# Indices of block 2 transposed earlier, block 3's weights ordered behind block 4's dots, two small loads moved to POOL

## The chip, the cores and the metric

The kernel runs on one core of a Trainium2 chip. The metric is the time of one execution in device microseconds, median of three runs. The engines are TensorE (PE), VectorE (DVE), ScalarE (ACT), GpSimd (POOL) and SyncE (SP). Each works through its own instructions in a fixed order and waits where an input or a buffer isn't ready; everything behind a waiting instruction waits with it. Sixteen DMA engines move what the queues of SP, ACT and POOL issue.

## The reference, cut to what matters

One layer of a hybrid decoder for 512 prompt tokens and 8 samples. Two token mixers come first and are not touched. Behind them stands a channel mixer, PEER, and the change lies wholly in it. For each token and each of 8 heads it picks 16 of 16384 experts, so 128 a token:

```python
s1, i1 = lax.top_k(s[:, :, 0], 16); s2, i2 = lax.top_k(s[:, :, 1], 16)   # two key halves
eidx = i1 * 128 + i2                       # best 16 pairs a head, 128 experts a token
g    = softmax(top_s)
act  = gelu(einsum('nd,nhkd->nhk', x, u[eidx]))          # a dot with 128 rows of u
y    = x1 + einsum('nhk,nhkd->nd', g * act, v[eidx])     # a weighted sum of 128 rows of v
```

All is float32, a row of `u` or `v` is 4 KB, and `u` and `v` hold 64 MB each.

## The kernel before, in words

The prompt's 512 tokens make four blocks of 128: blocks 1 and 2 (`halves[0]`, in the code also A) and blocks 3 and 4 (`halves[1]`, also B). The part that matters here runs from about 1075 us to the end and has these pieces:

- **Gather and dot** (`gather_dot`, L1107 to L1122). For each k of 128, POOL issues an indirect DMA that fetches one row of `u` for each of the 128 tokens (512 KB, tile `urow`, L1115), and DVE takes the dot with the token's own row `xn2` (L1122) into column k of `S`. `urow` comes from a ring of 6 slots. `xn2` has one buffer, so block 4's can only be loaded (on SP's queue, L1110) once block 3's last dot is done. `gelu_w` (L1132 to L1138) then turns `S` into weights.
- **Weights as a matrix** (`w_block`, L1161 to L1192). For blocks 1 to 3, rows of `v` are not gathered. The 128 weights of each token are spread over all 16384 experts: per token one one-hot over `i1` scaled by the weight and one over `i2`, and their product on PE gives a 128 x 128 table `WT`. 32 groups of 4 tokens; in each DVE makes `ohe` (L1173), DVE and POOL scale it (`oh`, L1178, L1176), ACT makes the other one-hot (L148, L1183), PE multiplies (`ps_w`, L1190), and ACT copies to `WT` (L151). Ahead of the groups `w_prep` (L1146) transposes `i1`, `i2` and `S` on PE (L1150) and copies them with ACT to `T_i1`, `T_i2`, `T_n2` (negated) and `T_S`, one buffer each. Block 3's `WT` tiles take the slots of block 1's.
- **Dense passes** (`v_part`, L1194 to L1200). SP loads 128 rows of `v` at a time (`vtile`, 512 KB, 5 slots) and PE multiplies them with `WT`. Pass 1: row tiles 0 to 63 for block 1. Pass 2: 64 to 127 for blocks 1 and 2. Pass 3: 0 to 63 for blocks 2 and 3. Pass 4: 64 to 127 for block 3. After the last matmul of a block `v_done` (L1203) adds the residual `x1r` on DVE (L1207) and stores.
- **Block 4 by gather** (`v_rows_acc`, L1210 to L1218). Beside passes 3 and 4, POOL gathers block 4's rows of `v` (L1214, tiles `vslab` and `vrow`) and DVE adds them into an accumulator (L1216), which lies in lane 0 of `slab[0]` and starts as the residual, loaded on SP's queue (L1211). The first 32 rows alternate between ring slots and 7 lanes of the slab.
- **Samples** (`sample_peer`, L1220 to L1263). The 8 samples' dots (`urow_s`, `xb`) are strewn among block 4's, their `v` rows (`vrow_s`) among block 4's rows. Their residual `x1s` takes one of the five `v` slots (L1259), is loaded by SP (L1260), added and stored.

Program order and engine order are not the same. A planner fixes each engine's order when the kernel is built: it plays the program through with durations of its own and lets each engine take the first ready instruction in program order. `tc.issue_after(x)` lets those instructions of its body which are on the engine of x follow x. Before, pass 1 carries such an anchor: block 2's `w_block` stays behind the matmuls of row tile 27 on PE (`JW`), and block 4's rows follow its last `urow` on POOL. On the chip the order stays, while the durations differ from the planner's.

The order of the program around the change: `w_block` of block 1, the top-16 search of block 4 (`late`), gather of block 3 with pass 1, `w_block` of block 2, pass 2, gather of block 4, `w_block` of block 3, pass 3, pass 4 with block 4's rows.

Of the kernel before, what the change touches and what calls it, by code (L numbers as in the profile page):

```python
# [15 lines left out]
P = 128  # L16
# [35 lines left out]
BPE, NPE = (4, 4), (4, 2)  # L52
EQD = (5, 6)
EARLY = True
JH, JC, JW = 64, 0, 27
SLOPES = [2.0 ** (-(h + 1)) for h in range(8)]


def step_kernel(
# [1048 lines left out]
    def gather_dot(d, tok, off, steps, every):  # L1108
        xn2 = keep.tile([P, D], F32, tag="xn2", name="xn2", bufs=1)
        nc.sync.dma_start(xn2, scr_xn2[tok:tok + P])  # L1110
        for k in range(P):
            if steps and k % every == 0:
                next(steps, None)
            gt = ring.tile([P, D], F32, tag="g", name="urow")
            d["rows"] = nc.gpsimd.indirect_dma_start(  # L1115
                out=gt, out_offset=None, in_=u_rows,
                in_offset=bass.IndirectOffsetOnAxis(ap=d["e"][:, k:k + 1], axis=0))
            if off and k % off == off - 1:
                nc.gpsimd.tensor_mul(gt, gt, xn2)
# [23 lines left out]
    def w_new(*pools):  # L1143
        return [(pool.tile([P, JH, P], F32, tag="WT", name="WT", bufs=2), JH * i) for i, pool in enumerate(pools)]

    def w_prep(sel, pool, pst_):  # L1146
        out = []
        for key in ("i1", "i2", "S"):
            p = pst_()
            nc.tensor.transpose(p[:, 0:P], sel[key], ident)  # L1150
            t = pool.tile([P, P], BF16 if key == "i1" else F32, tag=f"T_{key}", name=f"T_{key}", bufs=1)
            copy(t, p[:, 0:P])
            out.append(t)
            if key == "i2":
                t = pool.tile([P, P], F32, tag="T_n2", name="T_n2", bufs=1)
                copy(t, p[:, 0:P], scale=-1.0)
                out.append(t)
        return out

    iota4 = []  # L1160

    def w_block(sel, wT, pool, pst_, no):
        ONA, PM = ONAS[no], PMS[no]
        if not iota4:
            t = pool.tile([P, P, TG], BF16, name="iota4")
            nc.vector.tensor_copy(t, iota.unsqueeze(2).to_broadcast([P, P, TG]))
            iota4.append(t)
        i1T, i2T, ni2T, sT = w_prep(sel, pool, pst_)
        for g in range(P // TG):
            t0 = g * TG  # L1170
            tg = slice(t0, t0 + TG)
            e = pool.tile([P, P, TG], BF16, tag="ohe", name="ohe", bufs=OHE)
            nc.vector.tensor_tensor(e, iota4[0], i1T[:, tg].unsqueeze(1).to_broadcast([P, P, TG]), op=ALU.is_equal)  # L1173
            a = pool.tile([P, TG, P], F32, tag="oh1", name="oh1", bufs=OH1)
            sb = sT[:, tg].unsqueeze(2).to_broadcast([P, TG, P])
            nc.gpsimd.tensor_mul(a[:, :PM], e.rearrange("p j t -> p t j")[:, :PM], sb[:, :PM])  # L1176
            if PM < TG:
                nc.vector.tensor_mul(a[:, PM:], e.rearrange("p j t -> p t j")[:, PM:], sb[:, PM:])  # L1178
            b = pool.tile([P, TG, P], F32, tag="oh2", name="oh2", bufs=OHB)
            for t in range(ONA):  # L1180
                act(b[:, t, :], iota, AF.Abs, bias=ni2T[:, t0 + t:t0 + t + 1])
            if ONA:
                nc.scalar.activation(b[:, 0:ONA, :], b[:, 0:ONA, :], AF.Relu, bias=one, scale=-1.0)  # L1183
            if ONA < TG:
                n = TG - ONA
                nc.vector.tensor_tensor(b[:, ONA:TG, :], iota.unsqueeze(1).to_broadcast([P, n, P]),
                                        i2T[:, t0 + ONA:t0 + TG].unsqueeze(2).to_broadcast([P, n, P]), op=ALU.is_equal)
            pw = pst_().rearrange("p (t j) -> p t j", t=TG)
            for t in range(TG):
                nc.tensor.matmul(pw[:, t, :], b[:, t, :], a[:, t, :], start=True, stop=True)  # L1190
            for w, j0 in wT:
                copy(w[:, :, t0:t0 + TG], pw[:, :, j0:j0 + w.shape[1]].rearrange("p t j -> p j t"))  # L1192

    def v_part(j, use):  # L1194
        vt = dv[0].tile([P, D], F32, tag="v", name="vtile", bufs=VB)
        nc.sync.dma_start(vt, v_rows[j * P:(j + 1) * P])
        for py, wT, j0, j1 in use:
            w = next(w[:, j - b, :] for w, b in wT if b <= j < b + w.shape[1])
            for q in range(2):
                mm = nc.tensor.matmul(py[q], w, vt[:, q * 512:(q + 1) * 512], start=(j == j0), stop=(j == j1))  # L1200
        return mm

    def v_done(tok, py):  # L1203
        t = dv[0].tile([P, D], F32, tag="v", name="x1r", bufs=VB)
        nc.sync.dma_start(t, scr_x1[tok:tok + P])
        for q in range(2):
            nc.vector.tensor_add(t[:, q * 512:(q + 1) * 512], t[:, q * 512:(q + 1) * 512], py[q])  # L1207
        nc.scalar.dma_start(y_prompt[0, tok:tok + P], t)

    def v_rows_acc(d, tok, acc, slot):  # L1210
        nc.sync.dma_start(acc, scr_x1[tok:tok + P])  # L1211
        for k in range(P):
            gt = slot()
            nc.gpsimd.indirect_dma_start(out=gt, out_offset=None, in_=v_rows,  # L1214
                                         in_offset=bass.IndirectOffsetOnAxis(ap=d["e"][:, k:k + 1], axis=0))
            nc.vector.scalar_tensor_tensor(acc, gt, d["S"][:, k:k + 1], acc, op0=ALU.mult, op1=ALU.add)  # L1216
            yield
        nc.gpsimd.dma_start(y_prompt[0, tok:tok + P], acc)  # L1218

    def sample_peer(py):  # L1220
# [30 lines left out]
        for b in range(NS):  # L1251
# [15 lines left out]
    for hf in range(2):  # L1267
# [50 lines left out]
        if hf == 1:  # L1318
            alt = [0]

            def pst_w():
                alt[0] ^= 1
                return pst("ao"[alt[0]])

            wA0 = w_new(wr, wr)
            w_block(halves[0][0][0], wA0, wr, pst_w, 0)
            late()
            py = []
            steps = sample_peer(py)
# [100 lines left out]
```

## Time and profile before

| | us |
|---|---|
| median of 3 runs | 2266.93 (2264.25 to 2271.74) |
| the profiled execution | 2271.8 |
| its span | 2270.1 |
| PE, DVE, POOL, ACT busy | 1977.4, 1536.7, 1307.7, 655.4 |
| mean DMA rate over the span | 310 GB/s |

The profile is of one execution. Times in its rows count from the start of the span. A "DMA share" is the mean busy share of the 16 DMA engines; where they are never idle it reads 1.03. In brackets behind an instruction stands how long its engine was idle before it, and what ended that. A float32 matmul appears as two records.

### The profile page before, as it was taken

What the parts mean: (1) busy time and instruction counts of PE and PEld (TensorE: products, weight loads), DVE (VectorE), ACT (ScalarE), POOL (GpSimd) and SP (SyncE); (2) the same over time, 40 slices, a digit from 0 to 9 for tenths busy, and PEclk for the clock granted to TensorE, in tenths of its full rate; (3) what the DMA queues carried; (4) which work ended last, traced back from release to release, by engine and by line L of the source; (5) the groups of instructions that cost most, each with busy time, mean ns of one, the idle gap of its engine ahead of it and who ended that gap; (6) DMA issues with size and microseconds to landing.
All of it is one profiled execution on the core that took longest, in us unless ns stands there. A gap on an engine that the chain in (4) does not pass through costs nothing. (4 is left out here: it accounts for less than half of the span.)

```text
span 2270.1 us, 25459 instructions
## 1 busy us (share of the span) xinstructions
PE 1977.4 (87%) x7694; PEld 1312.6 (58%) x7694; DVE 1536.7 (68%) x3504; ACT 655.4 (29%) x1775; POOL 1307.7 (58%) x1226
## 2 busy tenths in 40 slices
PE   6999999888989999899897984989999699986817
PEld 4675777777878777787775732634445544431202
DVE  2355576787698977777886698855626856536694
ACT  3343233311344433334534315910014600000000
POOL 0487783453486645676776377554415854545573
PEclk9997999999988999999997997999999699997959
DMA  5685776889698889999988297899969899999999
GB/s 158 199 271 203 236 242 214 276 281 325 221 323 286 299 280 340 343 355 340 325 313 321 87 347 262 309 380 409 409 238 355 279 404 409 409 376 417 417 392 369
DMA packets 297803, 704.78 MB, mean 310 GB/s; under 512 B 31518, under 2 KB 157530, under 8 KB 297666
## 3 DMA queue, kind: packets, MB, share of 16 engines
q0 software_dynamic: 114224, 415.84, 49.1%
q1 hardware_dynamic: 183010, 285.74, 35.8%
q10 hardware_dynamic: 432, 1.57, 0.2%
q8 instruction: 61, 1.00, 0.2%
q14 instruction: 76, 0.62, 0.1%
HBM read 684.87 MB, written 18.18 MB: 310 GB/s over the span
## 5 line engine op out<-in xcount | busy, mean ns | idle before, releaser
L1115 POOL DMA_INDIRECT urow<-in_peer_u,k_e x512 | 602.2, 1176 | 394.9 <-DVE urow L1122 279.5
L1122 DVE SCALAR_TENSOR_TENSOR urow<-urow,xn 128x1024 f32<-128x1024 f32 x512 | 643.7, 1267 | 176.4 <-DMA urow<-in_peer_u,k_e 171.7
L1200 PE MATMUL y<-vtile,WT 128*128 128x512 f32 x1024 | 467.4, 601 | 73.6 <-DMA vtile<-in_peer_v 73.1
L291 PE MATMUL ps_mm<-x,wch 128*128 128x264 f32 (+1 forms) x1536 | 384.0, 403 | 27.5 <-DVE sig L315 20.2
L1200 PEld LDWEIGHTS y<-vtile,WT 128*128 128x128 f32 x1024 | 192.2, 192 | 337.5 <-issue 230.2
L291 PEld LDWEIGHTS ps_mm<-x,wch 128*128 128x128 f32 x1536 | 300.4, 200 | 83.9 <-DVE sig L315 23.5
L835 POOL TENSOR_TENSOR kpage<-kpage,qb 128x1024 f32<-128x1024 f32 x64 | 150.2, 2360 | 72.1 <-DMA qb<-scr_q 64.7
L291 PE MATMUL ps_mm<-hT,wch 128*128 128x256 f32 (+1 forms) x768 | 184.8, 390 | 3.9 <-DVE sig L315 3.6
L1214 POOL DMA_INDIRECT vslab<-in_peer_v,k_e x112 | 131.6, 1175 | 87.2 <-DMA vslab<-in_peer_v,k_e 37.7
L1216 DVE SCALAR_TENSOR_TENSOR vslab<-vslab,k_S 128x1024 f32<-128x1024 f32 x112 | 143.9, 1285 | 44.6 <-DMA vslab<-in_peer_v,k_e 41.9
L291 PEld LDWEIGHTS ps_mm<-hT,wch 128*128 128x128 f32 x768 | 143.1, 193 | 26.4 <-DVE sig L315 4.0
L1200 PE MATMUL ps_a<-vtile,WT 128*128 128x512 f32 x256 | 135.4, 611 | 18.4 <-DMA vtile<-in_peer_v 18.3
L296 PE MATMUL ps_mm<-wch,x 128*128 128x256 f32 (+1 forms) x640 | 150.0, 386 | 0.0
L823 POOL DMA_INDIRECT vpage<-in_cache_v,kidx x64 | 79.1, 1236 | 107.6 <-DVE vacc L901 68.1
L1200 PE MATMUL ps_o<-vtile,WT 128*128 128x512 f32 x256 | 132.3, 599 | 0.0
L296 PEld LDWEIGHTS ps_mm<-wch,x 128*128 128x128 f32 (+1 forms) x640 | 108.0, 174 | 29.5 <-issue 2.8
L901 DVE SCALAR_TENSOR_TENSOR vacc<-vpage,aS,vacc 128x128 f32<-128x128 f32 x384 | 110.6, 359 | 18.6 <-DMA vpage<-in_cache_v,kidx 18.4
L148 ACT ACTIVATE oh<-iota,T_n 128x128 f32<-128x128 f32 x352 | 113.4, 403 | 0.1
L1190 PE MATMUL ps_w<-oh,oh 128*128 128x128 f32 x512 | 81.1, 313 | 31.6 <-POOL oh L1176 23.9
L1190 PEld LDWEIGHTS ps_w<-oh,oh 128*128 128x128 f32 x512 | 74.3, 219 | 52.1 <-POOL oh L1176 33.6
L1176 POOL TENSOR_TENSOR oh<-ohe,T_S 128x128 f32<-128x128 bf16 (+1 forms) x96 | 69.7, 733 | 53.2 <-ACT T_S L151 37.3
L836 DVE TENSOR_REDUCE sK<-kpage 128x16 f32<-128x1024 f32 x64 | 77.3, 1211 | 29.1 <-POOL kpage L835 29.0
(428 smaller groups left out, 2728.1 us busy)
## 6 DMA issues: line engine op xcount, KB each, us to landing
vtile<-in_peer_v SPq DMA_DIRECT2D x256, 512.0 KB
wch<-in_w_in SPq DMA_DIRECT2D x256, 256.0 KB
wch<-in_peer_wq SPq DMA_DIRECT2D x64, 256.0 KB
wch<-in_w_branch_a SPq DMA_DIRECT2D x32, 256.0 KB
wch<-in_w_branch_b SPq DMA_DIRECT2D x32, 256.0 KB
wch<-in_w_out SPq DMA_DIRECT2D x32, 256.0 KB
urow<-in_peer_u,k_e POOLq DMA_INDIRECT x512, 7.9
qb<-scr_q SPq DMA_DIRECT2D x8, 512.0 KB
```

The source lines that it names most:

```text
L148: nc.scalar.activation(out, in_, func, bias=b[:n, 0:1] if b.shape[0] != n else b, scale=scale, **kw)
L291: nc.tensor.matmul(out, w[:, c0:c0 + m], xk[:, :n], start=(k == 0 and i == 0), stop=(k == KT - 1 and i == len(tt) - 1))
L296: nc.tensor.matmul(out, x[:, k, t0:t0 + m], ch[k // KP][:, k % KP, :n], start=(k == 0), stop=(k == KT - 1))
L823: nc.gpsimd.indirect_dma_start(out=t, out_offset=None, in_=rows, in_offset=bass.IndirectOffsetOnAxis(ap=kidx[:, b * 8 + pg:b * 8 + pg + 1] ...
L835: (nc.vector if KDV and pg % KDV == KDV - 1 else nc.gpsimd).tensor_mul(kt, kt, qb)
L901: nc.vector.scalar_tensor_tensor(acc[:, h, :], vt[:, h, :], wa, acc[:, h, :], op0=ALU.mult, op1=ALU.add)
L1115: d["rows"] = nc.gpsimd.indirect_dma_start(out=gt, out_offset=None, in_=u_rows, in_offset=bass.IndirectOffsetOnAxis(ap=d["e"][:, k:k + 1], ...
L1122: d["dot"] = nc.vector.scalar_tensor_tensor(gt, gt, 1.0, xn2, op0=ALU.mult, op1=ALU.mult, accum_out=d["S"][:, k:k + 1])
L1190: nc.tensor.matmul(pw[:, t, :], b[:, t, :], a[:, t, :], start=True, stop=True)
L1200: mm = nc.tensor.matmul(py[q], w, vt[:, q * 512:(q + 1) * 512], start=(j == j0), stop=(j == j1))
L1214: nc.gpsimd.indirect_dma_start(out=gt, out_offset=None, in_=v_rows, in_offset=bass.IndirectOffsetOnAxis(ap=d["e"][:, k:k + 1], axis=0))
L1216: nc.vector.scalar_tensor_tensor(acc, gt, d["S"][:, k:k + 1], acc, op0=ALU.mult, op1=ALU.add)
```

## The change

- `w_prep` takes a list of what to transpose and keeps the results in the block's record; the tiles have two buffers each. `T_n2` is gone: ACT computes |i2 - iota| with scale -1 and bias `T_i2` in place of |iota - i2|.
- Block 2's three transposes stand right behind block 1's `w_block` (so ahead of `late` and of pass 1's anchor). Block 3's `i1` and `i2` stand ahead of block 4's gather; its `S` stays in `w_block`.
- Block 3's `w_block` gets two anchors: its DVE instructions follow block 4's dot 24, its POOL instructions follow block 4's gather 30 (both counted from 0).
- Block 4's accumulator is a tile of its own in the buffer of `xn2`, loaded by POOL. The samples' `x1s` is a tile of the ring, loaded by POOL.
- The split between passes is named `NA` (64) and no longer `JH` (64).

```diff
-JH, JC, JW = 64, 0, 27
+JH, JC, JW, NA, HB = 64, 0, 27, 64, (24, 30)
...
-    def w_prep(sel, pool, pst_):
-        out = []
-        for key in ("i1", "i2", "S"):
+    def w_prep(sel, pool, pst_, keys=("i1", "i2", "S")):
+        T = sel.setdefault("T", {})
+        for key in keys:
             p = pst_()
             nc.tensor.transpose(p[:, 0:P], sel[key], ident)
...
+            T[key] = pool.tile([P, P], BF16 if key == "i1" else F32, tag=f"T_{key}", name=f"T_{key}", bufs=2)
+            copy(T[key], p[:, 0:P])
...
-        i1T, i2T, ni2T, sT = w_prep(sel, pool, pst_)
+        w_prep(sel, pool, pst_, [k for k in ("i1", "i2", "S") if k not in sel.get("T", {})])
+        i1T, i2T, sT = (sel["T"][k] for k in ("i1", "i2", "S"))
...
-                act(b[:, t, :], iota, AF.Abs, bias=ni2T[:, t0 + t:t0 + t + 1])
+                act(b[:, t, :], iota, AF.Abs, scale=-1.0, bias=i2T[:, t0 + t:t0 + t + 1])
...
     def v_rows_acc(d, tok, acc, slot):
-        nc.sync.dma_start(acc, scr_x1[tok:tok + P])
+        nc.gpsimd.dma_start(acc, scr_x1[tok:tok + P])
...
-        x1s = dv[0].tile([NS, D], F32, tag="v", name="x1s", bufs=VB)
-        nc.sync.dma_start(x1s, scr_x1s)
+        x1s = ring.tile([NS, D], F32, tag="g", name="x1s")
+        nc.gpsimd.dma_start(x1s, scr_x1s)
...
             w_block(halves[0][0][0], wA0, wr, pst_w, 0)
+            w_prep(halves[0][0][1], wr, pst_w)
             late()
...
     v_done(0, useA0[0])
+    w_prep(selB[0], wr, pst_d, ("i1", "i2"))
     gather(1, 1, lambda: wr.tile([P, P], F32, name="ge_y", bufs=1),
            (next(steps) if k % 8 == 4 and k < 68 else None for k in range(P)))
     wB0 = w_new(wr, wr)
-    w_block(selB[0], wB0, wr, pst_d, 2)
+    with tc.issue_after(selB[1]["dots"][HB[0]].ins), tc.issue_after(selB[1]["gets"][HB[1]].ins):
+        w_block(selB[0], wB0, wr, pst_d, 2)
...
-    run = v_rows_acc(selB[1], HALF + P, slab[0][:, 0, :], gslot)
+    acc = keep.tile([P, D], F32, tag="xn2", name="acc", bufs=1)
+    run = v_rows_acc(selB[1], HALF + P, acc, gslot)
```

## Rows read from the trace of the kernel before

**Rows 1.** Windows: us, busy time by engine (instructions), PE clock, DMA share, GB/s.
```profile
1380.00:1400.00 20.00, 4.60 (x7) 2.15 (x8) 13.53 (x31) 8.58 (x26) 17.38 (x18) 0.52 0.47 148
...
1660.00:1670.00 10.00, 10.00 (x24) 4.37 (x23) 0.00 (x0) 0.00 (x0) 0.00 (x0) 1.00 0.53 190
1670.00:1680.00 10.00, 10.00 (x25) 4.43 (x24) 0.00 (x0) 0.00 (x0) 0.00 (x0) 1.00 0.43 152
1680.00:1690.00 10.00, 10.00 (x26) 4.45 (x25) 0.43 (x1) 0.28 (x1) 0.38 (x1) 1.00 0.54 205
1690.00:1700.00 10.00, 10.00 (x37) 5.46 (x36) 7.80 (x14) 4.21 (x12) 5.07 (x6) 1.00 0.42 140
...
1960.00:2000.00 40.00, 40.00 (x95) 17.72 (x94) 22.19 (x40) 1.61 (x4) 24.90 (x23) 1.00 1.03 413
...
2080.00:2120.00 40.00, 35.29 (x72) 12.05 (x71) 35.96 (x28) 0.00 (x0) 25.28 (x21) 0.93 1.03 419
...
2260.00:2265.00 5.00, 5.00 (x13) 2.09 (x11) 0.30 (x1) 0.00 (x0) 0.59 (x1) 1.00 0.54 217
2265.00:2270.00 5.00, 0.52 (x2) 0.00 (x0) 1.08 (x2) 0.00 (x0) 0.00 (x0) 0.98 0.26 105
```

**Rows 2.** Timeline of PE around the transposes of block 2.
```profile
1367.02 0.38 PE L1150 MATMUL ps_w<-ident,k_i 128*128 128x128 f32 x2
1395.40 0.47 PE L1150 MATMUL ps_w<-ident,k_S 128*128 128x128 f32 x1 [28.00 <-ACT T_i L151]
...
1406.55 2.05 PE L1190 MATMUL ps_w<-oh,oh 128*128 128x128 f32 x16 [1.85 <-POOL oh L1176]
```

**Rows 3.** Timelines of DVE: last top-16 work of block 4; block 3's first one-hot.
```profile
1396.99 0.69 DVE L1021 TENSOR_REDUCE k_i<-tk_eq 128x32 f32<-128x512 f32 x1 [2.14 <-POOL tk_eq L1017]
...
1481.78 0.76 DVE L1173 TENSOR_TENSOR ohe<-iota,T_i 128x512 bf16<-128x512 bf16 x2 [5.68 <-ACT T_i L151]
```

**Rows 4.** Timelines of DVE, POOL and ACT where block 4's dots would start.
```profile
1689.57 1.23 DVE L1178 TENSOR_TENSOR oh<-ohe,T_S 128x384 f32<-128x384 bf16 x2 [34.24 <-ACT T_S L151]
...
1689.62 1.43 POOL L1176 TENSOR_TENSOR oh<-ohe,T_S 128x128 f32<-128x128 bf16 x2 [37.30 <-ACT T_S L151]
...
1689.26 0.28 ACT L151 ACTIVATE T_S<-ps_w 128x128 f32<-128x128 f32 x1 [34.58 <-PE ps_w L1150]
```

**Rows 5.** Timeline of SP's queue in pass 2.
```profile
1627.34 51.83 SPq L1196 DMA_DIRECT2D vtile<-in_peer_v  x16
1679.22 0.42 SPq L1110 DMA_DIRECT2D xn<-scr_xn  x1
```

**Rows 6.** Timeline of DVE: block 4's dots 0 and 15, one sample's, the next one-hot.
```profile
1695.46 1.21 DVE L1122 SCALAR_TENSOR_TENSOR urow<-urow,xn 128x1024 f32<-128x1024 f32 x1
...
1724.99 1.23 DVE L1244 SCALAR_TENSOR_TENSOR urow_s<-urow_s,xb 128x1024 f32<-128x1024 f32 x1 [3.93 <-DMA xb<-scr_xn2s]
1726.89 1.23 DVE L1122 SCALAR_TENSOR_TENSOR urow<-urow,xn 128x1024 f32<-128x1024 f32 x1 [0.67 <-DMA urow<-in_peer_u,k_e]
1728.96 1.23 DVE L1122 SCALAR_TENSOR_TENSOR urow<-urow,xn 128x1024 f32<-128x1024 f32 x1 [0.83 <-DMA urow<-in_peer_u,k_e]
...
1732.81 1.28 DVE L1122 SCALAR_TENSOR_TENSOR urow<-urow,xn 128x1024 f32<-128x1024 f32 x1 [0.24 <-DMA urow<-in_peer_u,k_e]
1734.03 1.41 DVE L1178 TENSOR_TENSOR oh<-ohe,T_S 128x384 f32<-128x384 bf16 x2
```

**Rows 7.** Timeline of PE: end of pass 2; start of pass 3.
```profile
1729.47 1.02 PE L1200 MATMUL ps_o<-vtile,WT 128*128 128x512 f32 x2
...
1810.89 9.58 PE L1200 MATMUL y<-vtile,WT 128*128 128x512 f32 x20 [0.47 <-ACT WT L151]
```

**Rows 8.** Timelines of DVE and POOL: last dot, first row, end of pass 3.
```profile
1989.92 1.23 DVE L1122 SCALAR_TENSOR_TENSOR urow<-urow,xn 128x1024 f32<-128x1024 f32 x1 [0.81 <-DMA urow<-in_peer_u,k_e]
...
1995.11 1.28 DVE L1216 SCALAR_TENSOR_TENSOR vslab<-vslab,k_S 128x1024 f32<-128x1024 f32 x1
...
2021.43 0.69 DVE L1207 TENSOR_TENSOR x1r<-x1r,y 128x512 f32<-128x512 f32 x1 [25.04 <-PE y L1200]
...
1979.30 0.94 POOL L1115 DMA_INDIRECT urow<-in_peer_u,k_e  x1 [0.94 <-DVE urow L1122]
1980.54 1.20 POOL L1214 DMA_INDIRECT vslab<-in_peer_v,k_e  x1 [0.30 <-issue]
```

**Rows 9.** What SP's queue waited for after 2100 us: total, times, longest.
```profile
SPq L1196 <- DMA out_y_sample<-x1s: 55.8, 1, 55.8
```

**Rows 10.** What the tile xb and its loads show, from its own view.
```profile
DMA to landing us min/median/max: 5.3/10.2/11.6
```

More of the change, by code (lines that the diff above doesn't have):

```diff
@@ L1117, in gather_dot @@
                 in_offset=bass.IndirectOffsetOnAxis(ap=d["e"][:, k:k + 1], axis=0))
+            d.setdefault("gets", []).append(d["rows"])
             if off and k % off == off - 1:
@@ L1123, in gather_dot @@
                                                           accum_out=d["S"][:, k:k + 1])
+                d.setdefault("dots", []).append(d["dot"])
     def gather(hf, i, y=None, steps=None, every=1):
@@ L1144, in w_new @@
         return [(pool.tile([P, JH, P], F32, tag="WT", name="WT", bufs=2), JH * i) for i, pool in enumerate(pools)]
-    def w_prep(sel, pool, pst_):
-        out = []
-        for key in ("i1", "i2", "S"):
+    def w_prep(sel, pool, pst_, keys=("i1", "i2", "S")):
+        T = sel.setdefault("T", {})
+        for key in keys:
             p = pst_()
             nc.tensor.transpose(p[:, 0:P], sel[key], ident)
[L1151 to L1158, printed above, removed]
+            T[key] = pool.tile([P, P], BF16 if key == "i1" else F32, tag=f"T_{key}", name=f"T_{key}", bufs=2)
+            copy(T[key], p[:, 0:P])
     iota4 = []
@@ L1332, in step_kernel @@
             with tc.issue_after(sel[1]["score"].ins):
-                mms = [v_part(j, [useA0]) for j in range(JH)]
+                mms = [v_part(j, [useA0]) for j in range(NA)]
         if hf == 0 and SV == 1:
@@ L1358, in v_acc @@
         return [dps.tile([P, 512], F32, tag=f"y{b}{q}", name=f"y{b}{q}") for q in range(2)]
-    useA1 = (v_acc(1), wA1, JH, JH - 1)
-    for j in range(JH, P):
+    useA1 = (v_acc(1), wA1, NA, NA - 1)
+    for j in range(NA, P):
         v_part(j, [useA0, useA1])
     v_done(0, useA0[0])
+    w_prep(selB[0], wr, pst_d, ("i1", "i2"))
     gather(1, 1, lambda: wr.tile([P, P], F32, name="ge_y", bufs=1),
@@ L1366, in step_kernel @@
     wB0 = w_new(wr, wr)
-    w_block(selB[0], wB0, wr, pst_d, 2)
+    with tc.issue_after(selB[1]["dots"][HB[0]].ins), tc.issue_after(selB[1]["gets"][HB[1]].ins):
+        w_block(selB[0], wB0, wr, pst_d, 2)
     useB0 = (v_acc(2), wB0, JC, (JC - 1) % P)
-    for j in range(JH):
+    for j in range(NA):
         v_part(j, [useA1] + ([useB0] if j >= JC else []))
@@ L1381, in gslot @@
         return slab[i // 8][:, i % 8, :]
-    run = v_rows_acc(selB[1], HALF + P, slab[0][:, 0, :], gslot)
-    for j in [*range(JH, P), *range(JC)]:
+    acc = keep.tile([P, D], F32, tag="xn2", name="acc", bufs=1)
+    run = v_rows_acc(selB[1], HALF + P, acc, gslot)
+    for j in [*range(NA, P), *range(JC)]:
         v_part(j, [useB0])
```

## The prediction

> **What bounds the kernel now.** I read the windows first, for where the DMA engines stand still, then the timelines of the engines at those places, then what each queue waits for. Only the last 900 us matter, since nothing is changed ahead of them. In passes 3 and 4 the reader sees a DMA share of 1.03 at 413 to 419 GB/s [rows 1]: a transfer of 512 KB (a `vtile`, or one gathered row for 128 tokens) then costs 0.524 MB / 413 GB/s = 1.27 us, whoever issues it. PE is also full in pass 3 (95 records in 40 us, 0.42 us each), but pass 4 has only 64 x 4 records, 108 us of PE in the some 240 us from the end of pass 3 to the end of the run. So what ends last is the sum of bytes. An edit is worth the DMA idle time that it fills, provided no engine's order gives it back.
>
> DMA idle time at the places that the change touches, as 1.03 less the share [rows 1]: 1380 to 1400 us, 0.56 x 20 = 11.2 us; 1660 to 1700 us, (0.50 + 0.60 + 0.49 + 0.61) x 10 = 22.0 us; the last 10 us of the run, (0.49 + 0.77) x 5 = 6.3 us.
>
> **The change part by part**, against the profiled execution of 2271.8 us.
>
> *Block 2's indices ahead.* PE reaches the transposes at 1367 and stands for 28.00 us, until ACT has copied `T_i`, which lies behind block 4's top-16 work in ACT's order [rows 2]. That wait goes. What is late next is the same top-16 work: DVE ends it at 1397.7 [rows 3], and block 2's one-hots beyond the first buffers (two of the scaled kind) and ACT's copies to `WT` stand behind it. So PE gets two groups through, and a tile or two, and stands again until about 1397. The third group, now at 1406.55 [rows 2], then starts some 9 us earlier. Likewise DVE's 5.68 us for `T_i` of block 3 go [rows 3], since that one-hot now waits for dot 24. I count 6 us of earlier passes, from bounds of 0 (the same wait one instruction later) and 28 (the whole of it), and 3 us of filled DMA time from 0 to 11.2, nearer the low end because the empty stretch around 1390 stays. The three transposes and copies that move are 0.2 and 0.3 us each (two transposes in 0.38 us, a copy in 0.28 us [rows 2, 4]), under 2 us even if nothing hides them beside block 1's `w_block`. The scale of -1 replaces no instruction by a longer one, and three copies `T_n2` of 0.3 us go; both at nothing. `NA` equals `JH`.
>
> *Block 3's weights behind dot 24 and gather 30.* DVE and POOL stand for 34.24 and 37.30 us for `T_S`, whose transpose PE reaches only at 1689, and block 4's dots and gathers are queued behind [rows 4]. That is the 22 us hole. With the anchors no one-hot is ahead of the dots any more. What is late next is `xn2`: SP issues it at 1679.22, behind 16 tiles of pass 2 [rows 5]. A 512 KB load takes 5.3 us at the least [rows 10], so dot 0 could start at 1684, or 1678 with the 6 us above, against 1695.46 [rows 6]: 11.5 to 17.5 us of a 40 us hole that costs 0.55 us of DMA time a us, so 6.3 to 9.6 us. Upper bound 22 (`xn2` moves far forward in SP's order too). I take 9.
>
> The price: now the one-hots resume behind dot 15, at 1734.03 [rows 6], just as pass 2 ends its block 1 matmuls [rows 7], which frees block 3's `WT` slots. Behind dot 24 they come nine dots later. Dots 0 to 15 took 37.4 us, nine more at 2.07 us (1726.89 to 1728.96 [rows 6]) make 18.6, one more sample's dot 4 to 5. From 1678 that is 1738 to 1739, and with the three groups that were made in the hole before, at 1.2 us of DVE each, the phase stands 8 us further back than now. Against the 6 us gained before it, pass 3 starts 0 to 15 us later than 1810.89 [rows 7]; I take 3. POOL, DVE, ACT and PE all have one-hot work queued there, and PE's pass 3 waits for it. It costs little DMA time, because without tiles the dots go on at DVE's 1.3 us, near the DMA's 1.27; I take 1, from 0 to 8 (half of 15 us).
>
> *Accumulator in the buffer of `xn2`.* Its load must follow dot 127 and sits on POOL among the row gathers. From the last `urow` issue (1979.30) to the end of the last dot (1991.15) are 11.9 us, in which POOL now issues rows [rows 8]. If the planner puts the load right behind the last `urow`, these rows are 11 us late; if after a few rows, less. Since ring and slab hold only 13 rows, and these go out well before pass 3 ends, little is lost: 1 us, from 0 to 6 (half of 11.9). The Trainium skill (DMA: Bandwidth & Descriptors, "Anatomy of one DMA — SWDGE (gpsimd) path") says that any wait on a semaphore is made by the issuing sequencer before dispatch, not by the DMA engine, so a load that waits holds back all behind it on its queue. The 37.30 us of POOL agree [rows 4]. By that rule the move speaks against the change, as the fourth rival below.
>
> *`x1s` in the ring.* It holds one of five `v` slots until the samples' output has left, and SP's next tile waits 55.8 us for that [rows 9]. Meanwhile the gathers keep the DMA full, so the wait itself is worth nothing. But it pushes tiles to the very end, where PE runs on alone and the DMA idles for 6.3 us [rows 1]. I take 4, from 0 (the gathers end last instead, with a wait for one row, DVE's 1.3 us and the store) to 6.3.
>
> Sum: -3 - 9 + 1 + 1 - 4 = -14 us, so 2258 for the profiled execution. That one lies 4.9 us above the median of 2266.93; on the median's scale the forecast is 2253.
>
> **The rivals.** (a) *Given back at the end of pass 3.* DVE does one row, then stands 25.04 us for block 2's last matmul, because `v_done`'s adds come next in its order [rows 8]. If gathers end 17 us earlier while pass 3 ends 3 us later and the adds keep that place, DVE stands some 45 us, the 13 row slots fill, and the DMA idles in place of the hole. For it: that wait is there now. Against it: in the planner's time too block 3's weights move behind nine dots, so pass 3 ends later there and more rows should come ahead of the adds. Then the 9 us are lost: 2262.
>
> (b) *Slower: weights too late.* The mechanism is the anchor. If part one yields nothing, dot 0 starts at 1684 and dot 24 ends at 1745; POOL's part comes two dots later still (gather 30 needs the slot of dot 26), at 1749, 15 us behind 1734. All 32 groups then follow, so pass 3 starts and ends 15 to 19 us later. If in addition DVE stands at `v_done`'s adds until then, the rows cannot use that time, and the whole of it reaches the end: 2267 + 17 - 4 = 2280. It decides from the point where the anchor frees the one-hots over 10 us after pass 2's last block 1 matmul. For it: the present place, dot 15, is already level with that matmul [rows 6, 7]. Against: the hole of 40 us that the dots get back.
>
> (c) *More than counted.* All of PE's 28 us are filled with tiles, SP reaches `xn2` that much earlier, and the hole closes altogether: -11 - 22 - 4 = -37 us, 2230. For it: the two waits are one chain through SP and PE. Against: block 4's top-16 work, which doesn't move.
>
> (d) *POOL held by the accumulator.* The load lands right behind the last `urow` in POOL's order, and 11.9 us of row gathers are late at half of the DMA's rate; 6 us in place of 1, 2258 on the median's scale, or 2264 with half the gain of the hole lost as well.
>
> That the anchors don't act (the planner's order leaves other work ahead of the dots) ends near (a) as well, and I count it there.
>
> **How the numbers follow.** This kernel's measurement tells about 0.3%, 6.8 us, from no change: faster is below 2260.1, slower above 2273.7. Chances: forecast 0.40 (its own range 2245 to 2260), (a) 0.23 (2258 to 2270), (b) 0.16 (2268 to 2285), (c) 0.14 (2222 to 2245), (d) 0.07. Faster: nearly all of the forecast, 0.38, (c) 0.14, a fifth of (a) and half of (d), 0.08: 0.60. Slower: 0.14 of (b) and 0.02 of (a). The rest, 0.24, is the same. The range leaves out the ends of (b) and (c): 2228 to 2279.
>
> **What would show it.** Right: PE has no 28 us wait at an `L1150` transpose; no DVE or POOL wait for `T_S` ahead of block 4's dots; the first dot waits for `xn2` instead, within 10 us of SP's issue; the DMA hole shrinks from 40 us to some 25; several `L1216` rows stand ahead of the adds of `v_done`; SP has no wait for the samples' output; the run ends with the store of the accumulator and not with PE. Wrong: pass 3 starting after 1826, a DMA share below 0.8 for over 15 us at the end of pass 3, or a POOL wait of over 10 us at the accumulator's load.

## The result and the profile after

The changed kernel takes 2280.54 us (median of 20 runs, 2267.85 to 2300.09) beside 2270.43 us of the kernel before: a ratio of 1.0055, 95% interval 1.0032 to 1.0078. It is slower by some 12 us, where 14 us less were forecast. The profiled execution took 2284.77 us (span 2283.1) against 2271.8.

Windows of the kernel after (columns as in [rows 1]):

```profile
1660.00:1700.00 40.00, 40.00 (x96) 17.71 (x95) 4.52 (x7) 0.28 (x1) 2.71 (x2) 1.00 0.56 201
1700.00:1740.00 40.00, 40.00 (x95) 17.64 (x94) 19.58 (x35) 0.00 (x0) 17.62 (x18) 1.00 0.98 378
...
1800.00:1860.00 60.00, 38.05 (x154) 31.30 (x154) 55.04 (x101) 42.84 (x126) 52.19 (x52) 0.60 0.87 296
```

The same long windows of the kernel before:

```profile
1660.00:1700.00 40.00, 40.00 (x107) 18.71 (x106) 8.23 (x14) 4.48 (x13) 5.44 (x6) 1.00 0.48 172
1700.00:1740.00 40.00, 39.59 (x119) 19.55 (x118) 23.52 (x42) 7.49 (x23) 22.46 (x23) 1.00 1.01 395
...
1800.00:1860.00 60.00, 55.61 (x143) 27.72 (x144) 34.65 (x71) 7.58 (x22) 34.96 (x34) 0.91 0.99 377
```

By 1.03 less the share, the hole of 1660 to 1740 us costs 22.0 + 0.8 = 22.8 us before and 18.8 + 2.0 = 20.8 us after: it hardly shrank. From 1800 to 1860 us it is 2.4 us before and 9.6 us after. That window is PE's story: 55.61 us busy before, when pass 3 was running, and 38.05 us after, when block 3's weights were still being made. Summed in windows of 10 us from 1060 us to the end, the idle DMA time grew from 156.5 to 166.3 us, while the span grew by 13.0 us. Most of these 9.8 us lie ahead of block 4's last top-16 row: from that row to the end the mean DMA share is 0.95 in both kernels, over 873.1 and 881.7 us.

Timelines of PE, DVE, SP and POOL of the kernel after, at the places of [rows 2 to 7]:

```profile
1368.87 1.95 PE L1187 MATMUL ps_w<-oh,oh 128*128 128x128 f32 x16
1403.04 2.08 PE L1187 MATMUL ps_w<-oh,oh 128*128 128x128 f32 x8 [32.22 <-POOL oh L1173]
...
1401.43 0.69 DVE L1021 TENSOR_REDUCE k_i<-tk_eq 128x32 f32<-128x512 f32 x1 [2.15 <-POOL tk_eq L1017]
...
1503.77 187.08 SPq L1193 DMA_DIRECT2D vtile<-in_peer_v  x53
1690.90 0.42 SPq L1110 DMA_DIRECT2D xn<-scr_xn  x1
...
1695.48 1.23 DVE L1123 SCALAR_TENSOR_TENSOR urow<-urow,xn 128x1024 f32<-128x1024 f32 x1 [36.73 <-DMA xn<-scr_xn]
...
1732.70 0.69 DVE L1204 TENSOR_TENSOR x1r<-x1r,ps_a 128x512 f32<-128x512 f32 x1 [7.00 <-PE ps_a L1197]
...
1755.55 1.23 DVE L1123 SCALAR_TENSOR_TENSOR urow<-urow,xn 128x1024 f32<-128x1024 f32 x1 [0.36 <-DMA urow<-in_peer_u,k_e]
1756.70 1.09 DVE L1170 TENSOR_TENSOR ohe<-iota,T_i 128x512 bf16<-128x512 bf16 x3
...
1763.42 0.78 POOL L1173 TENSOR_TENSOR oh<-ohe,T_S 128x128 f32<-128x128 bf16 x2
1763.89 3.78 PE L1187 MATMUL ps_w<-oh,oh 128*128 128x128 f32 x16 [15.78 <-POOL oh L1173]
...
1856.83 9.75 PE L1197 MATMUL y<-vtile,WT 128*128 128x512 f32 x20 [0.47 <-ACT WT L151]
```

In the kernel before, DVE and PE at the same place:

```profile
1730.11 0.68 DVE L1207 TENSOR_TENSOR x1r<-x1r,ps_a 128x512 f32<-128x512 f32 x1
...
1732.05 1.95 PE L1190 MATMUL ps_w<-oh,oh 128*128 128x128 f32 x16
```

The reader is to see four things. The 28.00 us wait at block 2's transposes [rows 2] is gone, and PE waits 32.22 us a few instructions on, for a one-hot behind the same top-16 work. The 34.24 us wait for `T_S` [rows 4] is gone, but dot 0 waits 36.73 us for `xn2` and starts at 1695.48, as before (1695.46, [rows 6]). Then, between dots 11 and 12, stand the two adds that close block 1 (`x1r`, in `v_done`), and they wait for pass 2's last block 1 matmul; before, they stood between dots 13 and 14 and did not wait. Dot 24 comes at 1755.55, POOL's first one-hot at 1763.42, and pass 3 starts at 1856.83 against 1810.89 [rows 7].

DVE and POOL at the end of block 4's dots, and DVE at the end of pass 3, in the kernel after:

```profile
1978.09 1.23 DVE L1123 SCALAR_TENSOR_TENSOR urow<-urow,xn 128x1024 f32<-128x1024 f32 x1 [0.98 <-DMA urow<-in_peer_u,k_e]
1988.51 0.58 POOL L1208 DMA_DIRECT2D acc<-scr_x  x1 [1.21 <-issue]
2003.80 1.28 DVE L1213 SCALAR_TENSOR_TENSOR acc<-vslab,k_S,acc 128x1024 f32<-128x1024 f32 x1 [20.55 <-DMA acc<-scr_x]
...
2084.30 0.69 DVE L1204 TENSOR_TENSOR x1r<-x1r,y 128x512 f32<-128x512 f32 x1 [7.25 <-PE y L1197]
```

The last dot is 11.8 us earlier than before [rows 8], the rows run ahead of the end of pass 3, where only 7.25 us are left of the 25.04, and SP's 55.8 us wait [rows 9] does not occur. That goes some way to explain why 46 us at the start of pass 3 cost only some 12 at the end; no run takes it apart.

### The profile page after: what moved, and what is told of

Its sections match the earlier page's. It is cut to its first block, busy times and chain, and to the rows that moved or that the text cites. A ratio compares the mean times of both kernels' runs of the same rounds, so it can differ in the third digit from the quotient of the medians.

```text
span 2283.1 us, 25449 instructions
## 1 busy us (share of the span) xinstructions
PE 1995.7 (87%) x7694; PEld 1324.3 (58%) x7694; DVE 1537.6 (67%) x3504; ACT 654.6 (29%) x1772; POOL 1327.2 (58%) x1228
## 5 line engine op out<-in xcount | busy, mean ns | idle before, releaser
L291 PE MATMUL ps_mm<-x,wch 128*128 128x264 f32 (+1 forms) x1536 | 394.6, 411 | 29.3 <-DVE sig L315 17.9
L291 PEld LDWEIGHTS ps_mm<-x,wch 128*128 128x128 f32 x1536 | 307.9, 205 | 88.9 <-DVE sig L315 20.8
L1213 DVE SCALAR_TENSOR_TENSOR acc<-vslab,k_S,acc 128x1024 f32<-128x1024 f32 x112 | 143.9, 1285 | 95.3 <-DMA vslab<-in_peer_v,k_e 72.8
L1211 POOL DMA_INDIRECT vslab<-in_peer_v,k_e x112 | 141.4, 1262 | 97.5 <-DMA vslab<-in_peer_v,k_e 56.0
L1187 PE MATMUL ps_w<-oh,oh 128*128 128x128 f32 x512 | 93.9, 345 | 83.6 <-POOL oh L1173 71.0
L1187 PEld LDWEIGHTS ps_w<-oh,oh 128*128 128x128 f32 x512 | 84.6, 248 | 104.4 <-POOL oh L1173 89.2
L296 PEld LDWEIGHTS ps_mm<-wch,x 128*128 128x128 f32 (+1 forms) x640 | 108.3, 174 | 30.2 <-issue 2.8
L148 ACT ACTIVATE oh<-iota,T_i 128x128 f32<-128x128 f32 x352 | 113.9, 405 | 0.1
L1197 PEld LDWEIGHTS ps_a<-vtile,WT 128*128 128x128 f32 x256 | 46.1, 193 | 75.6 <-issue 40.2
```

The source lines that it names most:

```text
L291: nc.tensor.matmul(out, w[:, c0:c0 + m], xk[:, :n], start=(k == 0 and i == 0), stop=(k == KT - 1 and i == len(tt) - 1))
L296: nc.tensor.matmul(out, x[:, k, t0:t0 + m], ch[k // KP][:, k % KP, :n], start=(k == 0), stop=(k == KT - 1))
```

## The experiments

Profiled executions of these kernels end block 4's top-16 work (`L1021`) anywhere from 1383.9 to 1413.1 us, which is scatter from ahead of all that is compared here. So the table gives, beside the ratio to the kernel before (measured anew with each group of experiments, 2266 to 2271 us), times from marks inside one trace: dot 0 and the start of pass 3, counted from the first instruction behind block 3's last dot (`k_top<-k_S` on DVE; 1651.47 in the kernel before, 1654.90 in the kernel after), and the end of the span, counted from the start of that last `L1021`. The column "dots" has how many of block 4's 128 dots stand ahead of block 3's last scaled one-hot in DVE's order.

```
kernel           ratio, 95% interval        dot 0   pass 3   dots   end from top-16
before           1                           44.0    159.4    44     873.1
after            1.0055 (1.0032 to 1.0078)   40.6    201.9    68     881.7
a_no_anchor      1.0032 (1.0002 to 1.0062)   49.2    165.2    44     877.9
b_anchor         1.0119 (1.0082 to 1.0156)   30.8    198.7    68     904.4
a_xn2_act        1.0064 (1.0039 to 1.0089)   20.7    200.7    68     881.8
b_xn2_act        1.0002 (0.9975 to 1.0029)   43.7    157.7    44     872.2
a_hb10           1.0015 (0.9990 to 1.0040)   34.3    158.2    45     875.5
a_xn2_hb10       1.0012 (0.9982 to 1.0041)   17.7    159.7    45     873.2
a_x1s_undone     1.0133 (1.0100 to 1.0167)   41.2    203.0    68     901.8
a_acc_undone     1.0075 (1.0049 to 1.0102)   40.7    203.1    68     885.8
a_moves_undone   1.0180 (1.0150 to 1.0210)   43.4    208.0    68     906.4
a_prep_undone    1.0035 (1.0008 to 1.0063)   37.5    204.2    69     883.6
c20_26           0.9976 (0.9953 to 0.9999)   24.9    185.6    61     869.4
cp20_26          0.9980 (0.9955 to 1.0004)   14.2    176.7    61     863.3
```

**The anchors, taken out and put in alone.** `a_no_anchor` is the kernel after with

```diff
-    with tc.issue_after(selB[1]["dots"][HB[0]].ins), tc.issue_after(selB[1]["gets"][HB[1]].ins):
-        w_block(selB[0], wB0, wr, pst_d, 2)
+    w_block(selB[0], wB0, wr, pst_d, 2)
```

> The kernel after, with block 3's weights made without the two anchors (no wait for dot 24 and gather 30). Theory A (the anchors are what costs: they hold block 3's one-hots back to about 1757, pass 3 starts at 1857 instead of 1811, and the hole before dot 0 stays because xn2 lands at 1695 anyway): here pass 3 starts at 1808 to 1825, dot 0 again at 1690 to 1700, 28 to 34 us of waiting for T_S come back on DVE, and the time is that of the kernel before or a little less, 2262 to 2273 us. Rival B (the two moved loads or the indices made ahead cost it): time stays at 2278 to 2286 though pass 3 starts early.

Measured: 2274.82 us. DVE waits for `T_S` again and pass 3 is early:

```profile
1692.47 1.23 DVE L1175 TENSOR_TENSOR oh<-ohe,T_S 128x384 f32<-128x384 bf16 x2 [38.89 <-ACT T_S L151]
...
1814.98 8.85 PE L1197 MATMUL y<-vtile,WT 128*128 128x512 f32 x20 [0.47 <-ACT WT L151]
```

The trace is theory A's, with a wait 5 us longer than expected; the time is a little above its range and short of rival B's, and its interval overlaps that of the kernel after. So the trace, and not the time, shows what the anchors do here. Without the anchors the rest of the change gains nothing, and may cost a few us: `T_S` comes 5 us later behind block 3's dots than in the kernel before. Where the rest of the 7 us lies stays open.

`b_anchor` is the kernel before with the anchors alone (the two lists of dots and gathers, and the line above the other way round).

> The kernel before, with the two anchors alone (dot 24, gather 30); indices, accumulator load and samples' residuals as before. Theory A: dot 0 is not earlier than 1688 (xn2 on SP's queue takes the place of T_S), block 3's first scaled one-hot on POOL at 1750 to 1765, pass 3 starts at 1845 to 1860, time 2276 to 2286. Rival B (the loss is from the other parts): pass 3 late all the same, but time 2258 to 2270. My prediction on record would have dot 0 at 1684 and the first one-hot at 1738.

Measured: 2292.45 us, slower than theory A's range and slower than the whole change. DVE and PE:

```profile
1682.41 1.23 DVE L1123 SCALAR_TENSOR_TENSOR urow<-urow,xn 128x1024 f32<-128x1024 f32 x1 [26.92 <-DMA xn<-scr_xn]
1726.75 0.69 DVE L1209 TENSOR_TENSOR x1r<-x1r,ps_a 128x512 f32<-128x512 f32 x1 [12.99 <-PE ps_a L1202]
1747.28 1.09 DVE L1175 TENSOR_TENSOR ohe<-iota,T_i 128x512 bf16<-128x512 bf16 x3
...
1850.33 29.97 PE L1202 MATMUL y<-vtile,WT 128*128 128x512 f32 x67 [0.47 <-ACT WT L151]
...
2182.82 62.05 DVE L1218 SCALAR_TENSOR_TENSOR vslab<-vslab,k_S 128x1024 f32<-128x1024 f32 x47 [0.42 <-DMA vslab<-in_peer_v,k_e]
2244.78 1.27 DVE L1264 TENSOR_TENSOR x1s<-x1s,ps_w 8x512 f32<-8x512 f32 x2
2252.03 42.95 PE L1202 MATMUL y<-vtile,WT 128*128 128x512 f32 x96 [68.05 <-DMA vtile<-in_peer_v]
```

SP's queue in its waits after 1850 us (total, times, longest):

```profile
SPq L1198 <- DMA out_y_sample<-x1s: 74.4, 1, 74.4
```

Two readings. First, dot 0 starts at 1682.41, just where the prediction put it and against theory A's 1688, and still the first one-hot comes at 1747 and pass 3 at 1850: the dots reach `x1r` at 1713.8, stand 12.99 us for the end of pass 2, and only then go on to dot 24. Counted from block 3's last dot, dot 0 is 9.8 us earlier than in the kernel after and pass 3 only 3.2 us. So `xn2` is not what makes the weights late. Second, the end: the samples' adds (`x1s`) stand on DVE behind 47 rows, until then the vtile slot is taken, SP's queue stands 74.4 us, and PE runs 96 records of matmuls (42.95 us) alone at the end. The kernel after, with `x1s` in a ring slot, has not that tail.

**`xn2` on another queue.** Both kernels with

```diff
-        nc.sync.dma_start(xn2, scr_xn2[tok:tok + P])
+        (nc.scalar if tok == HALF + P else nc.sync).dma_start(xn2, scr_xn2[tok:tok + P])
```

> The kernel after, with block 4's xn2 alone issued on ACT's queue instead of SP's (there it stands behind block 4's top-16 work and ahead of the k_e of block 3, where ACT waits anyway; on SP it stands behind 53 vtiles of pass 2). Theory A (two waits stood one beside the other, T_S on PE's side and xn2 behind the vtiles on SP's; the change took away one): dot 0 moves from 1695.5 to 1658 to 1675, the first one-hot from 1757 to 1720 to 1738, pass 3 from 1857 to 1812 to 1835, DMA idle time of 1650 to 1700 from 19 us to 5 to 12, time 2255 to 2270. Rival C (DMA engines are full with pass 2's tiles then and the gathers, so a dot that starts earlier is given back): dot 0 early, time 2276 to 2286 as after.

> The kernel before, with block 4's xn2 on ACT's queue. Theory A (the other wait, T_S, stands there still): xn2 lands by 1675, but dot 0 stays at 1688 to 1697 behind DVE's wait for T_S, and the time stays within 0.3% of before, 2262 to 2274. Rival D (xn2 was the only wait that mattered, T_S hung on it in some way): dot 0 by 1680 and time 2255 to 2262.

Measured: 2280.92 us and 2268.45 us. DVE of `a_xn2_act`:

```profile
1679.97 1.23 DVE L1123 SCALAR_TENSOR_TENSOR urow<-urow,xn 128x1024 f32<-128x1024 f32 x1 [3.29 <-DMA xn<-scr_xn]
1736.10 0.69 DVE L1204 TENSOR_TENSOR x1r<-x1r,ps_a 128x512 f32<-128x512 f32 x1 [28.39 <-PE ps_a L1197]
1760.62 1.09 DVE L1170 TENSOR_TENSOR ohe<-iota,T_i 128x512 bf16<-128x512 bf16 x3
```

Its windows at the hole:

```profile
1660.00:1700.00 40.00, 40.00 (x94) 17.68 (x94) 14.51 (x27) 1.60 (x4) 14.54 (x13) 1.00 0.83 307
1700.00:1740.00 40.00, 40.00 (x95) 17.73 (x94) 7.43 (x13) 0.28 (x1) 5.06 (x6) 1.00 0.76 285
```

Theory A fails here. Counted from block 3's last dot, dot 0 is 20 us earlier than in the kernel after, and all of it is given back at `x1r`: the wait grows from 7.00 to 28.39 us and the first one-hot stays at 1760. The hole has only moved: 8.0 + 10.8 = 18.8 us of idle DMA time, against 20.8. Rival C's time came true, but not by its mechanism, since the DMA engines idle. In `b_xn2_act` `T_S` alone holds dot 0 (43.7 us behind block 3's last dot, 44.0 before), and nothing is gained, as expected:

```profile
1705.74 1.23 DVE L1178 TENSOR_TENSOR oh<-ohe,T_S 128x384 f32<-128x384 bf16 x2 [24.06 <-ACT T_S L151]
```

So three waits end within some 40 us, each hiding behind the one before it: `T_S`, `xn2`, and the end of pass 2 at `x1r`.

**The anchors ahead of `x1r`.** The kernel after with `HB = (10, 16)` in place of `(24, 30)`; and the same with `xn2` on ACT's queue.

> The kernel after, with the anchors at dot 10 and gather 16 instead of dot 24 and gather 30. In DVE's order the adds of block 1's end (x1r) stand between dot 11 and dot 12 and wait for the end of pass 2 (1727 to 1736 in all kernels); dot 24 is behind them, dot 10 ahead. Theory A (the anchor's price is that place behind x1r): block 3's first one-hot at 1718 to 1728, PE goes on with block 3's weights within 5 us of the end of pass 2, pass 3 starts at 1810 to 1825, time 2262 to 2275. Rival B (the weights are late because POOL or DVE has too much between dots, whatever the anchor): pass 3 at 1840 or later, time 2275 or more.

> The kernel after, with the anchors at dot 10 and gather 16 and block 4's xn2 on ACT's queue: both waits ahead of the dots gone, and the one-hots ahead of x1r. Theory A: dot 0 at 1675 to 1685 (as with xn2 on ACT's queue alone, 1679.97), first one-hot 1695 to 1712, pass 3 at 1810 to 1825, last dot by 1972, time 2250 to 2264, faster than before. Rival C (DMA engines, not these orders, set the end; what is early is given back at x1r's second place, where the row adds wait for the end of pass 3): 2264 to 2275.

Measured: 2272.45 us and 2271.11 us. `a_hb10`, DVE and PE:

```profile
1709.12 1.14 DVE L1170 TENSOR_TENSOR ohe<-iota,T_i 128x512 bf16<-128x512 bf16 x3
1722.11 0.69 DVE L1204 TENSOR_TENSOR x1r<-x1r,ps_a 128x512 f32<-128x512 f32 x1 [6.12 <-PE ps_a L1197]
1724.48 1.95 PE L1187 MATMUL ps_w<-oh,oh 128*128 128x128 f32 x16
1808.84 11.06 PE L1197 MATMUL y<-vtile,WT 128*128 128x512 f32 x20 [0.47 <-ACT WT L151]
```

With the first one-hots ready ahead of `x1r`, PE goes on 2.4 us after it, and pass 3 stands at 158.2 us, as before the change. Theory A's time holds, and the first one-hot comes even ahead of its 1718; that shows the price to be in where the anchor stands. Whether it is the place behind `x1r` or the 14 dots more ahead of the one-hots is not told apart, since the edit changes both: 45 dots stand ahead of the last one-hot here, 68 in the kernel after. In `a_xn2_hb10` dot 0 is at 17.7, but DVE then waits 27.97 us at `x1r`, pass 3 is no earlier (159.7), the last dot starts at 2004.67 and not by 1972, and the 2250 to 2264 us of theory A are missed for rival C's 2264 to 2275.

**The two moved loads.** The kernel after with `x1s` back, with the accumulator back, and with both:

```diff
-        x1s = ring.tile([NS, D], F32, tag="g", name="x1s")
-        nc.gpsimd.dma_start(x1s, scr_x1s)
+        x1s = dv[0].tile([NS, D], F32, tag="v", name="x1s", bufs=VB)
+        nc.sync.dma_start(x1s, scr_x1s)
```

```diff
-        nc.gpsimd.dma_start(acc, scr_x1[tok:tok + P])
+        nc.sync.dma_start(acc, scr_x1[tok:tok + P])
...
-    acc = keep.tile([P, D], F32, tag="xn2", name="acc", bufs=1)
-    run = v_rows_acc(selB[1], HALF + P, acc, gslot)
+    run = v_rows_acc(selB[1], HALF + P, slab[0][:, 0, :], gslot)
```

> The kernel after, with the accumulator's load back on SP into slab lane 0 and the samples' residuals (x1s) back on SP into a vtile slot; anchors and early indices stay. Theory A (with pass 3 45 us later, the x1s load in a vtile slot stops SP's tiles for 60 to 75 us in pass 4, and the 96 or so matmuls left behind it, 43 us of PE, set the end; the ring slot is worth that): 2286 to 2298, as with the anchors alone (2292), with PE ending last. Rival: these moves are worth nothing or cost, 2270 to 2281.

> The kernel after, with only the samples' residuals (x1s) back on SP in a vtile slot. Both loads undone together gave 2310 us, with a 68.5 us wait of PE for a tile in pass 4 and 96 matmuls behind it. Theory A (x1s in the vtile slot is the whole of it): 2300 to 2316, SP again waits 60 to 75 us for the samples' store and PE ends last. Rival (the accumulator's load on POOL is half of it): 2286 to 2298.

> The kernel after, with only the accumulator's load back on SP in slab lane 0. Theory A (the load on POOL has only cost: DVE's first row add waits 20.5 us for it at 1983 to 2004): first row add within 6 us of the last dot, time 2268 to 2281. Rival (it is the accumulator's move that the kernel after gains from): 2285 to 2300.

Measured: both 2310.58 us, `x1s` alone 2296.91 us, the accumulator alone 2286.05 us. `a_x1s_undone`, DVE and PE:

```profile
2181.14 59.40 DVE L1213 SCALAR_TENSOR_TENSOR acc<-vslab,k_S,acc 128x1024 f32<-128x1024 f32 x45 [0.41 <-DMA vslab<-in_peer_v,k_e]
2240.46 1.26 DVE L1259 TENSOR_TENSOR x1s<-x1s,ps_w 8x512 f32<-8x512 f32 x2
2248.25 40.44 PE L1197 MATMUL y<-vtile,WT 128*128 128x512 f32 x88 [65.94 <-DMA vtile<-in_peer_v]
```

And SP's queue in its waits after 1850 us:

```profile
SPq L1193 <- DMA out_y_sample<-x1s: 71.8, 1, 71.8
```

The tail of `b_anchor` is back, with 88 records of matmuls. The interval lies clear of the kernel after's: the ring slot is worth 1.0133 less 1.0055, 0.8% or 18 us, once pass 3 is late (expected were 2300 to 2316 us, so it need not be the whole of what both moves are worth; both undone are slower than the 2286 to 2298 us expected, and 0.5% slower than `x1s` alone by the ratios, but these intervals overlap). For the accumulator alone the interval overlaps that of the kernel after; its 2286.05 us lie above theory A's range, at the low end of the rival's, so the move may even help. In `a_acc_undone`, DVE:

```profile
1963.72 1.23 DVE L1123 SCALAR_TENSOR_TENSOR urow<-urow,xn 128x1024 f32<-128x1024 f32 x1 [0.82 <-DMA urow<-in_peer_u,k_e]
...
1968.91 1.28 DVE L1213 SCALAR_TENSOR_TENSOR vslab<-vslab,k_S 128x1024 f32<-128x1024 f32 x1
```

The first row add is 5.2 us behind the last dot, in place of 25.7, and the run is no shorter. DVE's wait for the accumulator costs nothing that shows.

**Block 2's indices inside its block again.** The kernel after without the early call:

```diff
-            w_prep(halves[0][0][1], wr, pst_w)
```

> The kernel after, with block 2's indices transposed inside its w_block again, not ahead. Theory A (the wait at the transposes was the same top-16 wait one instruction earlier): pass 2's first y between 1500 and 1512, no later than after's 1511.9; pass 2's end within 6 us of after's; time 2276 to 2286, unchanged. Rival (early indices put PE's, ACT's and DVE's orders out of step and cost): 2265 to 2275. Rival (they do gain): over 2288.

Measured: 2276.39 us, on theory A's edge. From the last top-16 row to pass 2's first `y` it is 108.3 us in the kernel before, 110.5 after, 113.1 here: the early indices bring pass 2 forward by 2.6 us at the most. The ratios of after and of this kernel overlap.

**All three waits taken away.** The kernel after with `xn2` on ACT's queue, `HB = (20, 26)`, and block 1's closing adds ordered behind dot 26; `cp20_26` is the same without the early indices.

```diff
-    v_done(0, useA0[0])
...
+    with tc.issue_after(selB[1]["dots"][26].ins):
+        v_done(0, useA0[0])
     wB0 = w_new(wr, wr)
```

> The kernel after with all three waits taken from the front of block 4's dots: xn2 on ACT's queue, block 1's closing adds (x1r) ordered behind dot 26 instead of dot 11, anchors at dot 20 and gather 26. Theory A (T_S, xn2 and the end of pass 2 stood in series; only with all three out do the dots run through): dot 0 at 1675 to 1685, dots go on to dot 20 without a wait over 6 us, DMA idle time of 1650 to 1740 falls from 20 us to 10 or less, block 3's weights begin within 8 us of the end of pass 2, pass 3 at 1812 to 1830, last dot by 1965, time 2245 to 2262, faster than before. Rival C (what the dots take of the DMA engines' time pass 2's tiles lose, and pass 2 ends later by as much): the end of pass 2 at 1745 or later, pass 3 at 1825 to 1840, time 2262 to 2275.

> As the kernel with all three waits taken away (xn2 on ACT's queue, x1r behind dot 26, anchors at dot 20 and gather 26), and block 2's indices transposed inside its w_block again. Theory A: within 0.3% of that one, 2243 to 2265, since the early indices gain nothing and cost nothing. Rival: the early indices cost 4 to 8 us (undoing them alone gave 2276 against 2281 for the kernel after), so this one is that much faster.

Measured: 2261.30 us and 2260.58 us beside 2268.18 us. `c20_26`, DVE and PE:

```profile
1675.04 1.23 DVE L1123 SCALAR_TENSOR_TENSOR urow<-urow,xn 128x1024 f32<-128x1024 f32 x1 [2.91 <-DMA xn<-scr_xn]
1725.35 1.09 DVE L1170 TENSOR_TENSOR ohe<-iota,T_i 128x512 bf16<-128x512 bf16 x3
1742.70 1.95 PE L1187 MATMUL ps_w<-oh,oh 128*128 128x128 f32 x16
1747.86 0.68 DVE L1204 TENSOR_TENSOR x1r<-x1r,ps_a 128x512 f32<-128x512 f32 x1
...
1835.79 8.85 PE L1197 MATMUL y<-vtile,WT 128*128 128x512 f32 x20 [0.47 <-ACT WT L151]
```

Its windows at the hole:

```profile
1660.00:1700.00 40.00, 40.00 (x95) 17.73 (x94) 16.57 (x29) 1.88 (x5) 15.02 (x14) 1.00 0.80 290
1700.00:1740.00 40.00, 39.51 (x92) 17.02 (x90) 21.32 (x37) 0.00 (x0) 17.72 (x18) 1.00 1.01 404
```

The dots now run from 1675 to the one-hots at 1725 without a wait at `x1r`, and the hole costs 9.2 + 0.8 = 10.0 us in place of 22.8. PE finds the one-hots ready when it comes to them, at 1742.70, where the kernel after waits 15.78 us. It comes late: pass 2's last matmul (its 64 tiles are 256 records of `y`) ends at 1734.10, which is 83.9 us behind block 3's last dot, 80.7 in the kernel before, and PE then takes four tiles of pass 3 for block 2 ahead of the one-hots, which the kernel before strews among them. So rival C's mechanism, pass 2 ending later, can be some 3 us of it. Pass 3 starts at 1835.79, later than theory A's 1812 to 1830 and 26 us later than before on the scale of one trace, though no dot waits at `x1r`: the place behind those adds is not the whole price. The last dot, at 1975.04, misses theory A's 1965; the time is in its range. `c20_26` is 0.24% faster than the kernel before (0.01 to 0.47%, so only just clear of no change) and, by the two ratios, 0.8% faster than the kernel after. `cp20_26` is the same within its interval, which includes no change, as theory A has it, so the early indices are worth nothing that these runs can tell.

## Why the prediction was wrong

The step that failed is the price of the anchor: "From 1678 that is 1738 to 1739 ... pass 3 starts 0 to 15 us later than 1810.89; I take 3". It starts 46 us later, 42.5 on the scale of one trace (159.4 to 201.9). Counted from block 3's last dot, block 1's adds end at the same place in both kernels (79.9 and 79.3 us), and the 42.5 us lie behind them, in three parts:

- Some 20 us: the one-hots resume 22.5 us behind the adds (1756.70), in place of 2.6 (1734.03), since dots 12 to 24 stand between.
- Some 9 us: PE went on with one-hots that lay ready, 2.0 us ahead of DVE's next; now it starts 7.2 us behind DVE's first, when POOL has its own, behind gather 30.
- Some 14 us: the making of the weights takes 92.9 us, from 1763.89 to 1856.83, against 78.8 from 1732.05 to 1810.89. The prediction took three groups of 1.2 us for this; in its trace four groups are scaled in the hole (1689.57 twice, 1693.59, 1694.78), and it counted no dot more beside them.

The same two stretches as windows, of the kernel after and of the kernel before:

```profile
1763.89:1856.83 92.94, 59.42 (x256) 51.63 (x256) 86.81 (x158) 71.41 (x211) 81.10 (x82) 0.61 0.85 289
...
1732.05:1810.89 78.84, 53.04 (x261) 43.01 (x259) 69.31 (x124) 65.39 (x195) 61.43 (x67) 0.75 0.83 290
```

DVE is busy for 86.81 of the 92.94 us, with 43 dots among the one-hots (53.8 us) where the kernel before had 32 (40.7 us). That DVE sets the pace there is argued from this; PE's lower granted clock, 0.61 for 0.75, is a rival that no run takes out. In all, 68 dots stand ahead of the last one-hot in DVE's order in place of 44, where the prediction counted nine more, and in the table pass 3 goes with that number: 158 to 165 us with 44 or 45 dots, 177 to 186 with 61, 199 to 208 with 68 or 69, wherever dot 0 is. No run changes the number without the place.

The count from dot 0 to dot 24 (37.4, 18.6 and 4 to 5 us) comes out in the kernel after, 60.1 us, but by luck: the wait of 7.00 us at `x1r` is made up by dots whose rows have landed meanwhile, 1.15 us each. There it is the start, 1695.48 for 1678, that fails. But 1678 would not have helped. The adds of `v_done`, in the kernel before, drew no attention because they showed no wait, as the dots came late there. With the dots moved ahead of the one-hots, dots 12 to 24 must come behind the end of pass 2, whenever dot 0 starts: `a_xn2_act`, with dot 0 20 us earlier, takes 79.5 us from dot 0 to dot 24, and pass 3 is no better.

Point by point:

- *DMA sets the end.* Not borne out us for us: from the last top-16 row on, the DMA share is 0.95 in both kernels, and `c20_26`, which fills 12.8 us of the hole's 22.8, ends only 3.7 us earlier than the kernel before by the same mark.
- *Block 2's indices, -3 us.* Nothing that shows. The lower bound ("the same wait one instruction later") is what happened: 32.22 us in place of 28.00.
- *The hole, -9 us.* 2.0 us by the windows (22.8 to 20.8). In the profiled execution dot 0 did not move, with two more tiles ahead of `xn2` in SP's order (120 for 118) and SP 11.7 us later there. In `b_anchor` it started at 1682.41, as the prediction's 1684. But the sum let the freed dots run on to the end of the hole, and they could not.
- *Accumulator, +1 us.* Not to be told from zero. DVE's 20.55 us wait for it is real and free: `a_acc_undone` takes it away and is no faster. POOL did not wait over 10 us at the load (1.21 us), so rival (d) fell; its second time should have been 2262 or 2263, since half the gain of the hole is 4.5 us. POOL's 37.30 us [rows 4], given there for a load that waits, are a one-hot's wait; a waiting load is SP's in [rows 9].
- *`x1s`, -4 us, from 0 to -6.3.* Mis-sized, on the good side: 18 us, give or take 9 by the two intervals. The bound came from the last 10 us of the kernel before, but the blocked vtile slot costs more when pass 3 is late, since the tiles held back are then run by PE alone at the end. Without this part the change would have been 1.3% slower.
- *Rival (a)* fell: the rows moved ahead of the adds that end pass 3, and DVE waits 7.25 us there. *(c)* fell with part one.
- *Rival (b)* named the mechanism, weights too late behind the anchor, and its deciding point, one-hots over 10 us behind pass 2's last block 1 matmul (measured 24 to 31 us: 1756.70 and 1763.42 against 1732.7). Its 2280 us are the measured 2280.5, but that is luck, since its sizes are not the measured ones: a delay of 42 us and not 15 to 19, and it did not reach the end whole, since DVE did not stand at block 2's adds.

## What to carry to other kernels

Before an instruction is moved ahead in an engine's order, list everything that stands in that order between its old place and its new use, also what shows no wait now: a wait of zero in the old trace may be one that an earlier wait hides. Count also what is strewn among the moved work, not only what stands ahead of it. Where several waits stand one behind another, taking one away only shows the next; here the small gain came when all were gone, in `c20_26`. And count a time from a mark inside each trace when profiled executions differ by more than the effect.

## What the runs showed beyond that

A wait on a queue has no fixed price. In the kernel before, SP's wait for the samples' store (55.8 us) leaves PE 16 records behind the last tile:

```profile
2258.39 7.13 PE L1200 MATMUL y<-vtile,WT 128*128 128x512 f32 x16 [0.53 <-DMA vtile<-in_peer_v]
```

When pass 3 came 43 us later, the wait of 71.8 us left 88 records, 40.44 us, with no other work beside them, and taking it away was worth 18 us.

The profiled executions spread by 29 us (1383.9 to 1413.1) at a mark ahead of which most of these kernels are alike, and what sets that spread was not looked into.
